# GpSimd takes part of the weight and activation scaling at the start of a hybrid encoder block

## The chip, the cores and the metric

One Trainium2 (trn2) chip, one core of it. The metric is the device time of one execution in microseconds (us); the kernel before takes 1410.32 us, the median of three runs.

## What is computed

One layer of a bidirectional encoder over 2048 tokens of width 1024: RMS norm, one input projection, a Fourier branch and a dilated-attention branch, and one output projection. The change touches only the operands of the input projection.

```python
def reference(x, norm_w, w_in, q_norm_w, k_norm_w, w_fourier, w_out):
    ...
    h = x.astype(jnp.float32)
    ...
        hn = rms_norm(h, norm_w)
        proj = hn @ w_in.astype(jnp.float32)
        u_f, g_f, q, k, v, g_a = jnp.split(proj, SPLIT_POINTS, axis=-1)
        ...
        mixed = jnp.concatenate([y_f, y_a], axis=-1) @ w_out.astype(jnp.float32)
        h = h + mixed
    return h.astype(x.dtype)
```

## The kernel before

The projection keeps float32 accuracy with pairs of float16 numbers. Each normalized x is split into a high half (its float16 rounding) and a low half (what the rounding left), each weight too, and a product is three float16 matmuls: high by high, low by high, high by low. An item of the projection is one tile of 128 tokens against one weight block of 384 columns: 8 chunks of the contracted width by 3 products, 24 matmuls (`inproj`, L303 to L316). There are 12 such blocks (units) of 16 items each; item `t` of unit `u` runs in turn `i = 16u + t` of one long loop, which also carries the attention of earlier units.

At the start all operands have to be made. `x_sq` (L184) sums the squares of a row of x on ScalarE, `x_rs` (L194) makes the reciprocal root with a chain of ten dependent, tiny VectorE instructions (L107 to L114), `x_hi` (L209) scales an x tile to its high half `xhl`, `x_lo` (L217) makes the low half on VectorE from the float32 tile and the high half, `x_tr` (L225) transposes on TensorE and `x_ev` (L233) copies the transposed halves into `xT`, by ScalarE where tile number plus half is even and by VectorE otherwise. From tile 4 on the low half is transposed by a DMA instead (`x_dt`, L237). `w_prep` (L255) finds a power of two for a weight block, makes its high half `wh[:, 0]` chunk by chunk (L289, ScalarE) and the low half `wh[:, 1]` from it (L291, VectorE). Square roots go one tile at a time for tiles 0 to 3 and for two tiles at once from tile 4 on (`xgrp`).

The order is written out by hand: each engine works off its instructions in the order in which the program issues them. In turns 0, 1 and 2 the loop prepares x tiles 2, then 3, then 4 and 5 (L1132); in later turns one tile, three ahead of the item. After the item's 24 matmuls, `q_raw` and `q_v` (L323 to L332) move its result out of PSUM by ScalarE and VectorE, and `q_ss` (L342) sums squares on VectorE. GpSimd has no work between its set-up and turn 7, when it begins to scale q and k (L364, L365). In turns 1 to 3 the small instructions of `gains` (L156 to L168) are woven into the same VectorE order.

Of the kernel before, what the change touches and what calls it, by code (L numbers as in the profile page):

```python
# [16 lines left out]
AF = mybir.ActivationFunctionType  # L17
OP = mybir.AluOpType
# [74 lines left out]
class Kernel:  # L93
# [115 lines left out]
    def x_hi(self, r):  # L209
        nc = self.nc  # L210
        t = self.xtl(r)
        ri = self.x_ri(r)
        hl = [self.wk.tile([128, D], F16, name="xhl", tag="pp", bufs=4) for _ in range(2)]
        self.XH[r] = hl
        nc.scalar.activation(hl[0], t, AF.Copy, scale=ri)

    def x_lo(self, r):  # L217
        nc = self.nc
# [36 lines left out]
    def w_prep(self, u, nxt=False):  # L255
        nc = self.nc
        n = sum(x[1] for x in self.segs(u))
        wr = [self.WL.pop((u, k))[:, :n] for k in range(KT)]
        V, A = nc.vector, nc.scalar
        am8 = self.sm.tile([128, KT + 2], F32, name="am8", bufs=2)  # L260
        am = am8[:, KT + 1:KT + 2]
        nc.gpsimd.memset(am8[:, KT:KT + 1], 2.0 ** -58)
        for k in range(KT):
            V.tensor_reduce(am8[:, k:k + 1], wr[k], AX.X, OP.max, apply_absolute_value=True)
            yield
        V.tensor_tensor(am8[:, :KT], am8[:, :KT], self.nw, OP.mult)
        V.tensor_reduce(am, am8[:, :KT + 1], AX.X, OP.max, apply_absolute_value=True)
        yield
        pm = self.psm.tile([128, 512], F32, name="pm", tag="m")
        nc.tensor.matmul(pm[:, :128], am.to_broadcast([128, 128]), self.idf, start=True, stop=True)  # L270
        yield
        sb = self.sm.tile([128, 4], F32, name="scb", tag="scb", bufs=17)
        nws = self.sm.tile([128, KT], F32, name="nws", bufs=2)
        V.tensor_reduce(sb[:, 2:3], pm[:, :128], AX.X, OP.max)
        self.pow2(sb[:, 2:3], sb[:, 1:2], sb[:, 0:1])
        V.tensor_scalar(nws, self.nw, sb[:, 0:1], 8.0, op0=OP.mult, op1=OP.mult)
        V.tensor_scalar(sb[:, 0:1], sb[:, 0:1], 8.0, None, op0=OP.mult)
        V.tensor_scalar(sb[:, 1:2], sb[:, 1:2], 1.0 / 16, None, op0=OP.mult)
        V.scalar_tensor_tensor(sb[:, 2:3], sb[:, 0:1], EPS, sb[:, 0:1], op0=OP.mult, op1=OP.mult)
        V.tensor_scalar(sb[:, 3:4], sb[:, 1:2], 0.5, None, op0=OP.mult)  # L280
        if u < len(self.units):
            c, sp = self.units[u]
            V.tensor_copy(self.IS[:, sp // 2, c, sp % 2], sb[:, 1:2].to_broadcast([128, 2]))
        wh = self.wp.tile([128, 2, KT, 384], F16, name="wh", tag="wh", bufs=2)
        self.W[u] = wh, sb
        yield
        for k in range(KT + 1):
            if k < KT:
                A.activation(wh[:, 0, k, :n], wr[k], AF.Copy, scale=nws[:, k:k + 1])  # L289
            if k:  # L290
                V.scalar_tensor_tensor(wh[:, 1, k - 1, :n], wr[k - 1], nws[:, k - 1:k], wh[:, 0, k - 1, :n],  # L291
                                       op0=OP.mult, op1=OP.subtract)
                if nxt:
                    self.WQ.append((u + 1, k - 1))
            yield
# [1016 lines left out]
```

## Time and profile before

| | |
|---|---|
| median of 3 runs | 1410.32 us (1410.22 to 1411.82) |
| the profiled execution's own time | 1410.9 us |
| its span in the trace | 1409.1 us |
| TensorE busy | 1381.4 us (98%) |
| VectorE busy | 992.7 us (70%) |
| ScalarE busy | 748.7 us (53%) |
| GpSimd busy | 459.7 us (33%) |

The span is the time between the first and the last instruction of the trace; the execution's own time has 1.8 us more around it. A share of busy time is an average over the whole span. The change works in its first 45 us alone, so the stretches there are to be read, and what each engine waits for at their ends.

### The profile page before, as it was taken

Reading aid. Unit: us, or ns where it says so; the run is one execution under the profiler, and the core shown is the slowest. Engines: PE = TensorE matmul, PEld = TensorE weight load, DVE = VectorE, ACT = ScalarE, POOL = GpSimd, SP = SyncE. Lnnn points to the kernel's source line nnn. Section 1 sums busy time; section 2 is a strip of 40 time slices with the busy share of each in tenths; the row PEclk is TensorE's granted clock in tenths of the full one; section 3 lists DMA queues with packets and bytes.
Section 4 is the critical chain, followed back from the end, with each engine's and each line's share of the span. In section 5 each row is a group of like instructions: output and inputs, shape, how many; then the busy total and the mean of one; then the engine's idle time right before and its main releaser. Section 6 shows DMA issues by size and latency. Waiting matters only on the chain.

```text
span 1409.1 us, 27788 instructions
## 1 busy us (share of the span) xinstructions
PE 1381.4 (98%) x9506; PEld 1020.7 (72%) x9506; DVE 992.7 (70%) x3167; ACT 748.7 (53%) x2095; POOL 459.7 (33%) x639
## 2 busy tenths in 40 slices
PE   5999999999999999999999999999999999899998
PEld 3666666667777777778888888844448688788887
DVE  7888888878878888888887777744398887711111
ACT  6867767676757666666666565645213235410010
POOL 0255445444444444454433343320000101411110
PEclk9999999999999999999999999999999999999999
DMA  6876877786776767687766564545432526353432
GB/s 225 204 134 127 153 121 142 127 143 132 141 132 124 149 119 155 118 152 120 144 115 130 97 132 96 136 108 145 164 103 92 149 76 254 111 148 116 112 113 82
DMA packets 426829, 188.13 MB, mean 134 GB/s; under 512 B 320128, under 2 KB 410432, under 8 KB 426176
## 3 DMA queue, kind: packets, MB, share of 16 engines
q1 hardware_dynamic: 398084, 173.37, 56.3%
q10 hardware_dynamic: 28604, 13.00, 3.8%
q8 instruction: 74, 1.21, 0.4%
q14 instruction: 67, 0.55, 0.1%
HBM read 68.18 MB, written 29.76 MB: 70 GB/s over the span
## 4 chain that ended last, share of the span: by engine, by line
PE 82%; DVE 6%; issue 3%; DMA 3%; POOL 3%; ACT 2%; SPq 1%; POOLq 0%; DVEq 0%; ACTq 0%
PE psq L312 43%; PE py L948 13%; PE psq L574 12%; PE psq L590 5%; PE pS L461 3%; PE po L527 2%; PE po L528 1%; PE pS L449 1%; DVE xhl L223 1%; POOL ph L509 1%; DMA qw<-qw 1%; PE pf L828 1%; DMA wor<-in_w_out_dram 1%; POOL hl L376 1%; PE ptr L795 0%
## 5 line engine op out<-in xcount | busy, mean ns | idle before, releaser
L312 PE MATMUL psq<-wh,xT 128*128 128x384 f16 x4608 | 787.0, 327 | 3.3 <-ACT wh L289 1.5
L312 PEld LDWEIGHTS <-xT 128*128 128x128 f16 x4608 | 540.3, 119 | 193.8 <-issue 4.6
L497 ACT ACTIVATE P<-pS,ob,kb 128x256 f32<-128x256 f32 (+1 forms) x384 | 199.4, 527 | 150.5 <-DVE ob L489 150.1
L509 POOL TENSOR_TENSOR ph<-P,ph 128x512 f16<-128x512 f32 x160 | 189.5, 1184 | 196.4 <-ACT ph L504 184.1
L948 PE MATMUL py<-wo,mx 128*128 128x512 f32 x768 | 180.1, 397 | 3.8 <-DVE mx L927 3.8
L365 POOL TENSOR_TENSOR qn<-qn,kb 128x128 f32<-128x128 f32 x192 | 85.6, 446 | 293.7 <-DVE qn L364 201.9
L948 PEld LDWEIGHTS py<-wo,mx 128*128 128x128 f32 x768 | 146.1, 190 | 37.6 <-DVE mx L927 4.2
L574 PE MATMUL psq<-xT,wh 128*128 128x512 f16 x768 | 168.9, 379 | 0.0
L479 DVE CUSTOM_DVE_ANT_0 pS<-pS,bt 128x256 f32<-128x256 f32 (+1 forms) x384 | 147.7, 385 | 27.3 <-PE pS L449 18.8
L376 POOL TENSOR_TENSOR hl<-qn,hl 128x256 f16<-128x256 f32 x192 | 133.4, 695 | 29.7 <-ACT hl L371 29.7
L574 PEld LDWEIGHTS <-wh 128*128 128x128 f16 x768 | 74.1, 98 | 87.0 <-issue 0.8
L951 DVE TENSOR_TENSOR xo<-xo,py 128x512 f32<-128x512 f32 x32 | 22.0, 686 | 144.1 <-PE py L948 144.1
L538 DVE TENSOR_REDUCE ob<-po 128x128 f32<-128x256 f32 (+1 forms) x160 | 75.2, 470 | 54.1 <-PE po L528 54.1
L504 ACT CAST ph<-P 128x512 f16<-128x512 f32 x160 | 99.1, 619 | 9.4 <-DMA wr<-in_w_in_dram 1.6
L371 ACT CAST hl<-qn 128x256 f16<-128x256 f32 x192 | 77.1, 402 | 47.3 <-POOL qn L365 37.5
L332 DVE TENSOR_TENSOR vt<-psq,vt 128x128 f16<-128x128 f32 x192 | 55.0, 286 | 62.0 <-ACT vt L331 61.8
L331 ACT CAST vt<-psq 128x128 f16<-128x128 f32 x192 | 51.2, 267 | 82.8 <-PE po L528 82.8
L291 DVE SCALAR_TENSOR_TENSOR wh<-wr,nws,wh 128x384 f16<-128x384 f32 x128 | 86.5, 682 | 5.5 <-ACT wh L289 5.5
L590 PE MATMUL psq<-wh,xT 128*128 128x256 f16 x768 | 84.3, 273 | 0.0
L926 ACT CAST mx<-ya 128x512 fp32r<-128x512 f16 x16 | 9.9, 620 | 137.5 <-PE py L948 131.6
L590 PEld LDWEIGHTS <-xT 128*128 128x128 f16 x768 | 75.1, 98 | 9.1
L323 ACT COPY raw<-psq 128x256 f32<-128x256 f32 x192 | 69.4, 361 | 21.8 <-PE psq L312 21.4
(165 smaller groups left out, 1773.2 us busy)
## 6 DMA issues: line engine op xcount, KB each, us to landing
wr<-in_w_in_dram SPq DMA_DIRECT2D x104, 192.0 KB, 2.9
ot<-O SPq DMA_DIRECT2D x16, 792.0 KB, 4.5
st<-st SPq DMA_DIRECT2D x96, 128.0 KB, 2.4
xs<-in_x_dram SPq DMA_DIRECT2D x16, 512.0 KB, 6.9
xo<-in_x_dram SPq DMA_DIRECT2D x16, 512.0 KB, 3.6
out_dram<-xo SPq DMA_DIRECT2D x15, 512.0 KB, 3.0
O<-ob ACTq DMA_DIRECT2D x108, 66.0 KB, 2.5
O<-ob ACTq DMA_DIRECT2D x32, 132.0 KB, 2.7
```

The lines of the kernel that those rows point to most:

```text
L291: V.scalar_tensor_tensor(wh[:, 1, k - 1, :n], wr[k - 1], nws[:, k - 1:k], wh[:, 0, k - 1, :n], op0=OP.mult, op1=OP.subtract)
L312: nc.tensor.matmul(ps[:, :384], self.xtile(j, k, c, t), wh[:, l, k, :384], start=n == 0, stop=n == 23)
L365: G.tensor_tensor(qn[:, 2:4], qn[:, 2:4], self.kf[:, h0:h0 + 2], OP.mult)
L371: self.nc.scalar.copy(hl.rearrange("p a h l d -> p (a h) l d")[:, :, 0], qn)
L376: self.nc.gpsimd.tensor_tensor(hv[:, :, 1], qn, hv[:, :, 0], OP.subtract)
L479: V.tensor_tensor_reduce(out=sS[:, h, cs], in0=ps[:, h, cs], in1=bs, scale=1.0, scalar=-3.0e38, op0=OP.add, op1=OP.max, accum_out=mx[:, e, ...
L497: self.nc.scalar.activation(P[:, h, cs], sS[:, h, cs], AF.Exp, bias=ob[:, e, 130 + h:131 + h], scale=self.om[:, h0 + h:h0 + h + 1], accum_ ...
L504: self.nc.scalar.copy(ph[:, 0], P)
L509: self.nc.gpsimd.tensor_tensor(ph[:, 1], P, ph[:, 0], OP.subtract)
L574: nc.tensor.matmul(ps, wh[:, l, k, col * 128:col * 128 + 128], self.xT[:, j, k, ch * 512:ch * 512 + 512], start=n == 0, stop=n == 23)
L590: nc.tensor.matmul(ps[:, j * 256:j * 256 + 256], self.xT[:, i, k, r * 128:r * 128 + 128], wh[:, l, k, 128:384], start=n % 24 == 0, stop=n ...
L948: nc.tensor.matmul(ps[nh], m[:, j, k], wo[nh][k][:, l], start=(j, l, k) == (0, 0, 4), stop=(j, k) == (1, 3))
```

## The change

Two of the places that make a high half get a second engine. In `x_hi`, tiles 2 to 5 are scaled by GpSimd and no longer by ScalarE. In `w_prep`, for unit 0 alone, the odd chunks (four of eight) are scaled by GpSimd. Sizes, types and results stay as they were, and nothing else is edited.

```diff
@@ x_hi
         self.XH[r] = hl
-        nc.scalar.activation(hl[0], t, AF.Copy, scale=ri)
+        if 2 <= r < 6:
+            nc.gpsimd.tensor_scalar(hl[0], t, ri, None, op0=OP.mult)
+        else:
+            nc.scalar.activation(hl[0], t, AF.Copy, scale=ri)
@@ w_prep
             if k < KT:
-                A.activation(wh[:, 0, k, :n], wr[k], AF.Copy, scale=nws[:, k:k + 1])
+                if u == 0 and k % 2:
+                    nc.gpsimd.tensor_scalar(wh[:, 0, k, :n], wr[k], nws[:, k:k + 1], None, op0=OP.mult)
+                else:
+                    A.activation(wh[:, 0, k, :n], wr[k], AF.Copy, scale=nws[:, k:k + 1])
```

The added lines move the numbers of later ones: L215, L223, L235, L289, L291, L364 before are L218, L226, L238, L295, L297, L370 after.

On GpSimd, from the set-up to the first scaling of q, the order before is this (`am` belongs to the search for the power of two, `qn` to q and k):

```order
masks.py:199 AFFINE_SELECT idf<-idf 128x128
L262 MEMSET am_160 128x1
L364 TENSOR_TENSOR qn<-raw,qny 128x256
L365 TENSOR_TENSOR qn<-qn,kb 128x128
L376 TENSOR_TENSOR hl<-qn,hl 128x4x64
```

and in the change:

```order
masks.py:199 AFFINE_SELECT idf<-idf 128x128
L265 MEMSET am_160 128x1
L293 TENSOR_SCALAR wh<-wr,nws 128x384 x4
L216 TENSOR_SCALAR xhl<-xs,xri 128x1024 x4
L370 TENSOR_TENSOR qn<-raw,qny 128x256
L371 TENSOR_TENSOR qn<-qn,kb 128x128
L382 TENSOR_TENSOR hl<-qn,hl 128x4x64
```

Eight instructions stand where there were none; the later ones follow in the same order.

On ScalarE, from the first weight chunk to item 0's `vt`, the order before is this (`xjk` is `x_sq`; the first `xhl` row is tile 1, the second tile 2):

```order
L289 ACTIVATE wh<-wr,nws 128x384 x2
L192 ACTIVATE xjk,xss<-xs 128x1024
L289 ACTIVATE wh<-wr,nws 128x384 x6
L215 ACTIVATE xhl<-xs,xri 128x1024
L192 ACTIVATE xjk,xss<-xs 128x1024
L235 COPY xT<-xps 128x8x128
L192 ACTIVATE xjk,xss<-xs 128x1024
L215 ACTIVATE xhl<-xs,xri 128x1024
L192 ACTIVATE xjk,xss<-xs 128x1024 x2
L323 COPY raw<-psq 128x256
L324 ACTIVATE sq<-psq 128x256
L331 CAST vt<-psq 128x128
```

and in the change:

```order
L295 ACTIVATE wh<-wr,nws 128x384
L192 ACTIVATE xjk,xss<-xs 128x1024
L295 ACTIVATE wh<-wr,nws 128x384 x3
L218 ACTIVATE xhl<-xs,xri 128x1024
L192 ACTIVATE xjk,xss<-xs 128x1024
L238 COPY xT<-xps 128x8x128
L192 ACTIVATE xjk,xss<-xs 128x1024 x3
L329 COPY raw<-psq 128x256
L330 ACTIVATE sq<-psq 128x256
L337 CAST vt<-psq 128x128
```

Four chunks and tile 2 are gone from ScalarE; item 0's `raw`, `sq` and `vt` stand behind one x tile less.

Further on ScalarE, from there to the copy of tile 3's low half into `xT`, the order before is this (`xhl` is tile 3, then tiles 4 and 5; the `xT` rows are tile 2's high half and tile 3's low half):

```order
L331 CAST vt<-psq 128x128
L215 ACTIVATE xhl<-xs,xri 128x1024
L235 COPY xT<-xps 128x8x128
L192 ACTIVATE xjk,xss<-xs 128x1024 x2
L323 COPY raw<-psq 128x256
L324 ACTIVATE sq<-psq 128x256
L331 CAST vt<-psq 128x128
L215 ACTIVATE xhl<-xs,xri 128x1024 x2
L235 COPY xT<-xps 128x8x128
```

and in the change:

```order
L337 CAST vt<-psq 128x128
L238 COPY xT<-xps 128x8x128
L192 ACTIVATE xjk,xss<-xs 128x1024 x2
L329 COPY raw<-psq 128x256
L330 ACTIVATE sq<-psq 128x256
L337 CAST vt<-psq 128x128
L238 COPY xT<-xps 128x8x128
```

Both `xT` copies move up directly behind `vt`, since tile 3 and tiles 4 and 5 are gone. The orders of VectorE and TensorE are the same in both kernels.

## Rows read from the trace of the kernel before

**Rows 1.** The page's head and its first part: busy time of each engine.

```profile
span 1409.1 us, 27788 instructions
PE 1381.4 (98%) x9506; PEld 1020.7 (72%) x9506; DVE 992.7 (70%) x3167; ACT 748.7 (53%) x2095; POOL 459.7 (33%) x639
```

**Rows 2.** Busy time of each engine in stretches from 15 to 60 us.

```profile
15.00:30.00 15.00, 12.71 (x76) 6.82 (x75) 13.16 (x50) 13.23 (x25) 0.00 (x0) 1.00 0.69 278
30.00:45.00 15.00, 13.38 (x106) 8.29 (x105) 12.80 (x48) 13.97 (x25) 0.00 (x0) 1.00 0.56 147
45.00:60.00 15.00, 15.00 (x112) 9.62 (x110) 13.37 (x47) 11.88 (x24) 5.00 (x7) 1.00 1.16 264
```

**Rows 3.** Timeline of TensorE and its weight loads: start, duration, [idle before, releaser].

```profile
31.88 0.34 PE L312 MATMUL psq<-wh,xT 128*128 128x384 f16 x1 [0.83 <-ACT xT L235]
37.97 1.96 PE L312 MATMUL psq<-wh,xT 128*128 128x384 f16 x11 [0.62 <-ACT xT L235]
42.57 1.82 PEld L312 LDWEIGHTS <-xT 128*128 128x128 f16 x12 [0.18 <-ACT xT L235]
45.06 4.06 PE L312 MATMUL psq<-wh,xT 128*128 128x384 f16 x24
```

**Rows 4.** What TensorE waited for from 45 to 1240 us: total, times, longest.

```profile
PE py L948 <- DVE mx L927: 3.8, 1, 3.8
PE pS L461 <- DMA qw<-qw: 3.1, 6, 0.6
PE po L527 <- DMA pt<-ph: 0.6, 1, 0.6
```

**Rows 5.** Timeline of VectorE, 15 to 37 us.

```profile
15.00 0.16 DVE L279 SCALAR_TENSOR_TENSOR scb<-scb 128x1 f32<-128x1 f32 x1
15.81 1.14 DVE L291 SCALAR_TENSOR_TENSOR wh<-wr,nws,wh 128x384 f16<-128x384 f32 x2
25.76 0.16 DVE L114 SCALAR_TENSOR_TENSOR xri<-xn1t,xri 128x1 f32<-128x1 f32 x1
27.14 1.28 DVE L223 SCALAR_TENSOR_TENSOR xhl<-xs,xri,xhl 128x1024 f16<-128x1024 f32 x1 [0.38 <-ACT xhl L215]
29.91 0.29 DVE L332 TENSOR_TENSOR vt<-psq,vt 128x128 f16<-128x128 f32 x1 [0.44 <-ACT vt L331]
30.18 0.21 DVE L156 TENSOR_TENSOR kw<-kw,kt 24x64 f32<-24x64 f32 x1
34.64 0.16 DVE L114 SCALAR_TENSOR_TENSOR xri<-xn2t,xri 128x2 f32<-128x2 f32 x1
35.71 0.16 DVE L112 SCALAR_TENSOR_TENSOR xn2t<-xn2t,xss 128x2 f32<-128x2 f32 x1
35.98 0.68 DVE L235 COPY xT<-xps 128x1024 f16<-128x1024 f16 x1
36.58 2.47 DVE L223 SCALAR_TENSOR_TENSOR xhl<-xs,xri,xhl 128x1024 f16<-128x1024 f32 x2
```

**Rows 6.** Timeline of ScalarE, 14 to 41 us.

```profile
14.82 1.12 ACT L289 ACTIVATE wh<-wr,nws 128x384 f16<-128x384 f32 x2 [2.31 <-DVE nws L276]
34.83 2.19 ACT L215 ACTIVATE xhl<-xs,xri 128x1024 f16<-128x1024 f32 x2 [0.22 <-DVE xri L114]
40.47 1.15 ACT L215 ACTIVATE xhl<-xs,xri 128x1024 f16<-128x1024 f32 x1 [0.80 <-PE xps L230]
```

**Rows 7.** GpSimd and VectorE side by side at 75 us.

```profile
75.20 0.60 POOL L364 TENSOR_TENSOR qn<-raw,qny 128x256 f32<-128x256 f32 x1
75.29 0.54 DVE L112 SCALAR_TENSOR_TENSOR xn2t<-xn2t,xss 128x2 f32<-128x2 f32 x1
```

**Rows 8.** GpSimd's groups by shape: busy us, mean ns of one.

```profile
L509 POOL TENSOR_TENSOR ph<-P,ph 128x512 f16<-128x512 f32 x160 | 189.5, 1184 | 196.4 <-ACT ph L504 184.1 <-issue 10.0 <-DMA O<-ob 2.3
L365 POOL TENSOR_TENSOR qn<-qn,kb 128x128 f32<-128x128 f32 x192 | 85.6, 446 | 293.7 <-DVE qn L364 201.9 <-DVE qny L114 65.6 <-DVE qnt L110 21.2
L262 POOL MEMSET am<- 128x1 f32 x16 | 1.6, 97 | 0.0
masks.py:199 POOL TENSOR_SCALAR_AFFINE_SELECT idf<-idf 128x128 f32<-128x128 f32 x1 | 0.3, 292 | 0.1
masks.py:197 POOL MEMSET idf<- 128x128 f32 x1 | 0.2, 204 | 0.3 <-POOLq L1302 0.3
```

## The prediction, made before the changed kernel ran

> **What bounds the kernel now.** I read the engines' shares first, then the stretches of the start, then what TensorE waits for, and last VectorE's and ScalarE's timelines up to 45 us. TensorE is busy 98% of the span [rows 1] and from 45 us on in every microsecond: 15.00 of 15 [rows 2]. Behind that point it waits only for short things that are themselves paced by the items (3.8, 3.1 and 0.6 us in all) [rows 4]. So whatever the start loses or wins by the moment item 4 begins, at 42.57 us [rows 3], is carried to the end one to one.
>
> Before that moment TensorE waits, and the last to end each wait is a copy into `xT` by ScalarE: 0.83 us at 31.88, 0.62 at 37.97, 0.18 at 42.57 [rows 3]. That speaks for taking work from ScalarE, which is busy 13.23 and 13.97 of 15 us [rows 2]. But VectorE is as full, 13.16 and 12.80 of 15, and its few named waits for ScalarE in 15 to 37 us are 0.38 and 0.44 us [rows 5]. There are two bounds side by side, and the change relieves one of them.
>
> The reader should then look at how GpSimd and VectorE stand to each other. At 75 us GpSimd's L364 starts at 75.20 and ends at 75.80; VectorE's L112, tiny and 0.16 us long at 35.71 [rows 5], starts at 75.29 and takes 0.54 [rows 7]. Its own work thus began at 75.29 + 0.54 - 0.16 = 75.67, that is 0.13 us before GpSimd's end. VectorE instructions with two inputs in SBUF and GpSimd instructions exclude each other, from start to about 0.13 before the end. GpSimd has 0.00 us in 15 to 45 us now [rows 2], so VectorE is free of this there. All root chains, `x_lo` and the low halves of the weights are such two-input instructions.
>
> **The price of the new instructions.** No row shows GpSimd scaling one tensor by a column. From below: MEMSET, 97 ns for one column and 204 for 128 [rows 8], is 0.84 ns a column, so 0.42 us for 384 columns and 0.95 for 1024. From above: the two-input instruction, 446 ns for 128 columns and 1184 for 512 [rows 8], is 1.92 ns a column on a fixed 0.20, so 0.94 and 2.17. In between stands AFFINE_SELECT, one tensor in and one out, 292 ns for 128 columns: from MEMSET's 97 it is 1.5 ns a column, so 0.68 and 1.64; on the fixed 0.20 of the two-input line it is 0.7. I take 0.95 ns a column on 0.20, half of the two-input slope: t = 0.56 us for 384 and T = 1.2 us for 1024. ScalarE takes 2.19 for two of 1024 [rows 6], so the move itself costs next to nothing; the exclusion is the cost.
>
> The Trainium skill, GPSIMD Engine Reference, section 4.1, says that GpSimd's one-input elementwise instructions run at roughly line rate; with its 1.2 GHz that is an estimate of 0.85 us for 1024 columns, and with it the sum below would be about +0.7 us. The trace's AFFINE_SELECT, 0.7 to 1.5 ns a column, leaves it open; no other row here has one input.
>
> **The change, step by step,** as the delay of VectorE, which keeps its order.
>
> 1. Weight chunks. ScalarE's first two take 1.12 us from 14.82 [rows 6]; GpSimd's four start about 14.86, all inputs being there. L279 at 15.00 [rows 5] has two SBUF inputs and waits until 14.86 + 0.56 - 0.13 = 15.29: +0.29. The copy of `xT` behind it reads PSUM and runs beside chunk 3. The first low half, due at 15.81 + 0.29 = 16.10 [rows 5], meets chunk 5 (15.90 to 16.46) and starts at 16.33; chunk 7 goes between it and the second, which starts at 17.33 in place of 16.34. VectorE is **1.0 us** late. With t = 0.42 the same walk gives 0.4, with 0.94 it gives 2.3. ScalarE's four chunks less save nothing here: the root of tile 1 stands behind these low halves on VectorE.
>
> 2. Tile 2. Its root is ready at 25.92, the end of the L114 at 25.76 [rows 5]. GpSimd starts 0.07 later and holds VectorE until T - 0.06 behind the root. Three tiny two-input steps of tile 3's root stand ahead of `x_lo` and now come after, 0.58 us, so `x_lo` starts T + 0.52 behind the root. It was 27.14 - 25.92 = 1.22 [rows 5]. Late by T - 0.70 = **0.5**.
>
> 3. Tile 3. ScalarE, rid of tile 2, has `vt` ready early, so the 0.44 us wait before 29.91 [rows 5] falls away; `vt` reads PSUM and passes. Then L156, 30.18 [rows 5], waits for GpSimd until T - 0.06 behind tile 3's root, which is 29.91 - 0.44 = 29.47. Late by T - 0.77 = **0.43**, the gain of 0.44 already in it.
>
> 4. Tiles 4 and 5. The root is ready at 34.80, the end of the L114 at 34.64 [rows 5]. Two GpSimd instructions follow each other from 34.87 and hold VectorE's chain of the next root at two places; its L112, 35.71 [rows 5], starts at 34.70 + 2T. Late by 2T - 1.01 = **1.39**. The copy into `xT` behind it (35.98) and the two `x_lo` (36.58) are late by as much [rows 5].
>
> Together VectorE is 1.0 + 0.5 + 0.43 + 1.39 = 3.3 us late at 36 us. TensorE starts item 3 late by less, since ScalarE's copy is now early (the 0.62 wait at 37.97 goes). Item 4 hangs on tile 6's high half on ScalarE, which stands ahead of tile 4's copy there: it began at 40.47, 0.80 us of it waiting for TensorE [rows 6], while its root on VectorE came about 0.34 earlier. That slack is used up and 3.3 - 0.34 = **+3.0 us** is left. The transposing DMAs of the low halves follow `x_lo` and hide inside it. After item 4 nothing is added: the eight instructions are over before GpSimd's first old one, and TensorE sets the pace.
>
> The sum against the profiled execution is 1410.9 + 3.0 = 1413.9 us; the median of the runs is 0.6 below that execution, so 1413.3. With both prices at their lower ends it is 0.4 + 0.25 + 0.18 + 0.89 - 0.34 = +1.4, at the AFFINE_SELECT slope 1.3 + 0.94 + 0.87 + 2.27 - 0.34 = +5.0, at the two-input slope 2.3 + 1.47 + 1.4 + 3.33 - 0.34 = +8.2.
>
> **The rivals.**
>
> *VectorE is not held* (not slower). If a GpSimd instruction with one tensor input leaves VectorE its second reading port, or gives way at every meeting, only ScalarE's relief stays. Then VectorE wins 0.44 us at 29.91 and tile 3's copies no longer stand behind two high halves of 2.19 us [rows 6], but tile 6's root on VectorE, 0.34 before 40.47, then decides: -0.44 - 0.34 = -0.8 us, 1409.5. It decides from the point where the holds, 3.8 us in the sum above before the two gains of 0.44 and 0.34, fall under 0.8 us. For it: no row has a one-input GpSimd instruction beside a root chain. Against it: rows 7 show the hold plainly, and a read is a read.
>
> *Half of it is hidden.* GpSimd's chunks could fall beside the copy from PSUM and the single-input steps, and the two high halves of tiles 4 and 5 could hold at one place: steps 1 and 4 halve, 3.0 - 0.5 - 0.7 = +1.8 us, 1412.1.
>
> *GpSimd's pass is slow.* At T between 1.64 and 2.17 it is the price and not the meetings that counts, +5.0 to +8.2 us, 1415.3 to 1418.5. For it: every two-input row of GpSimd has this slope; against it: the instruction reads one tensor. The Trainium skill, same page, section 3.1, calls about 1.8 cycles an element the best case of a tight loop; at 1.2 GHz that is an estimate of 1.54 us for 1024 columns, and about +4.3 us by it. No run here shows this yet.
>
> **How the numbers follow.** A measurement of this kernel can tell about 0.2% from no change, 2.8 us. The forecast, holds with T from 0.95 to 1.64, gets 0.63; its middle, +3.0, is just above that line. Hidden by half gets 0.12, slow pass 0.12, not held 0.13. Of the forecast some 0.38 lies above 2.8 us, which with the slow pass makes slower 0.50. The rest of it, hidden and nearly all of not held make same 0.47; no case reaches -2.8, and 0.03 is left for what I overlook. The range runs from -0.8 (not held) to +5.7, between AFFINE_SELECT's slope and the slow pass's middle: 1409.5 to 1416.0, with about 0.1 left out above and less below.
>
> **What would show it.** GpSimd's four chunks near 0.56 us and four tiles near 1.2 us, longer where a VectorE instruction of two inputs runs; VectorE's second low half starting near 17.3, `x_lo` of tile 2 near 28.6, tile 3's copy by VectorE near 39.3; TensorE waiting at 32 and 37 us for VectorE and no longer for ScalarE; item 4 at about 45.6. An item 4 before 42 us, with root chains of undisturbed 0.16 us steps beside GpSimd, would make the forecast wrong; so would GpSimd tiles of 2 us, or new waits of TensorE behind 60 us.

## The result and the profile after

| | before | after |
|---|---|---|
| median of 5 runs of each, side by side | 1410.32 us (1410.22 to 1412.18) | 1418.38 us (1415.03 to 1420.14) |
| ratio | | 1.0051, 95% interval 1.0039 to 1.0063 |
| the profiled execution's own time | 1410.9 us | 1415.03 us |
| its span | 1409.1 us | 1413.2 us |
| item 4 starts | 42.57 us | 48.03 us |
| first weight scale `nws` starts | 14.55 us | 14.25 us |

The medians lie 8.1 us apart; the ratio of the runs makes the changed kernel slower by 0.51%, 7.2 us (5.5 to 8.9), where +3.0 us was forecast and the range ended at 1416.0. The profiled execution happens to be the quickest of its five runs. Executions start their first weight scale up to 1.2 us apart (14.22 to 15.40 us in the profiles of this study), so below the start of item 4 is counted from there: 28.02 us before, 33.78 after, **+5.76 us**.

The page's head and the stretches of the start, after (columns as in [rows 2]: stretch, its length, busy us and count of PE, PEld, DVE, ACT, POOL, then the granted clock, DMA share and GB/s):

```profile
span 1413.2 us, 27800 instructions
PE 1382.0 (98%) x9506; PEld 1020.2 (72%) x9506; DVE 997.9 (71%) x3167; ACT 743.3 (53%) x2087; POOL 479.3 (34%) x647
```

```profile
15.00:30.00 15.00, 12.39 (x60) 6.07 (x59) 12.78 (x42) 9.71 (x19) 7.76 (x5) 1.00 0.74 298
30.00:45.00 15.00, 11.72 (x98) 7.44 (x96) 12.57 (x43) 6.68 (x14) 8.55 (x3) 1.00 0.37 105
45.00:60.00 15.00, 13.04 (x97) 8.19 (x96) 12.18 (x46) 12.51 (x23) 2.86 (x3) 1.00 0.85 218
```

ScalarE went from 13.97 busy microseconds to 6.68 in the second stretch [rows 2], so it was relieved as meant. VectorE is hardly less busy than before and TensorE lost 1.66 us in that stretch. What follows 60 us did not change by more than execution to execution: TensorE's waits from 45 us on name the same tiles as [rows 4], with item 4's new wait among them.

GpSimd's groups by shape, after (busy us, mean ns of one):

```profile
L216 POOL TENSOR_SCALAR xhl<-xs,xri 128x1024 f16<-128x1024 f32 x4 | 11.4, 2853 | 12.1 <-DVE xss L200 6.7 <-DVE xri L114 5.5
L293 POOL TENSOR_SCALAR wh<-wr,nws 128x384 f16<-128x384 f32 x4 | 5.3, 1348 | 13.3 <-DMA xs<-in_x_dram 13.3
```

A tile takes 2.85 us and a chunk 1.35, against the 1.2 and 0.56 that I took, and above my upper bounds of 2.17 and 0.94 too.

GpSimd's timeline at the start, after (start, duration):

```profile
14.58 5.33 POOL L293 TENSOR_SCALAR wh<-wr,nws 128x384 f16<-128x384 f32 x4 [13.25 <-DMA xs<-in_x_dram]
26.60 2.85 POOL L216 TENSOR_SCALAR xhl<-xs,xri 128x1024 f16<-128x1024 f32 x1 [6.69 <-DVE xss L200]
32.06 2.87 POOL L216 TENSOR_SCALAR xhl<-xs,xri 128x1024 f16<-128x1024 f32 x1 [2.61 <-DVE xri L114]
37.76 5.68 POOL L216 TENSOR_SCALAR xhl<-xs,xri 128x1024 f16<-128x1024 f32 x2 [2.84 <-DVE xri L114]
```

VectorE's timeline beside it, after:

```profile
14.70 0.47 DVE L282 SCALAR_TENSOR_TENSOR scb<-scb 128x1 f32<-128x1 f32 x1
...
26.19 0.16 DVE L114 SCALAR_TENSOR_TENSOR xri<-xn1t,xri 128x1 f32<-128x1 f32 x1
...
26.82 0.91 DVE L110 TENSOR_TENSOR xn1t<-xri 128x1 f32<-128x1 f32 x1
27.76 0.16 DVE L112 SCALAR_TENSOR_TENSOR xn1t<-xn1t,xss 128x1 f32<-128x1 f32 x1
27.95 0.16 DVE L114 SCALAR_TENSOR_TENSOR xri<-xn1t,xri 128x1 f32<-128x1 f32 x1
29.48 1.28 DVE L226 SCALAR_TENSOR_TENSOR xhl<-xs,xri,xhl 128x1024 f16<-128x1024 f32 x1 [1.37 <-POOL xhl L216]
...
32.70 0.50 DVE L110 TENSOR_TENSOR xn2t<-xri 128x2 f32<-128x2 f32 x1
...
34.95 1.28 DVE L226 SCALAR_TENSOR_TENSOR xhl<-xs,xri,xhl 128x1024 f16<-128x1024 f32 x1 [0.46 <-POOL xhl L216]
...
38.23 0.67 DVE L110 TENSOR_TENSOR xn2t<-xri 128x2 f32<-128x2 f32 x1
...
40.66 2.13 DVE L226 SCALAR_TENSOR_TENSOR xhl<-xs,xri,xhl 128x1024 f16<-128x1024 f32 x1 [0.76 <-POOL xhl L216]
43.48 1.28 DVE L226 SCALAR_TENSOR_TENSOR xhl<-xs,xri,xhl 128x1024 f16<-128x1024 f32 x1 [0.69 <-POOL xhl L216]
44.68 0.15 DVE L110 TENSOR_TENSOR xn2t<-xri 128x2 f32<-128x2 f32 x1
```

Two different things are to be seen. First the **hold**: L110 at 26.82 takes 0.91 where the same step takes 0.16 undisturbed, so its own work began at 26.82 + 0.91 - 0.16 = 27.57, 0.97 us behind GpSimd's start. But GpSimd goes on until 29.45, and the two-input steps at 27.76 and 27.95 run beside it, undisturbed. The hold covers only the first third of the instruction. At L282, beside a chunk, the same reckoning gives 14.70 + 0.47 - 0.16 - 14.58 = 0.43 us. Second the **late result**: VectorE then has nothing to do but wait for the high half, 1.37, 0.46, 0.76 and 0.69 us before the four `x_lo`, each of which starts within 0.06 us of a GpSimd end. That is 3.28 us in all; before, only 0.38 us of such waiting stood there, for ScalarE at tile 2 [rows 5].

TensorE's timeline, after (the counterpart of [rows 3]; item 4 is the 48.03):

```profile
34.56 1.96 PE L318 MATMUL psq<-wh,xT 128*128 128x384 f16 x11 [1.00 <-DVE xT L238]
...
39.95 2.12 PE L318 MATMUL psq<-wh,xT 128*128 128x384 f16 x12 [0.59 <-DVE xT L238]
...
43.50 0.62 PE L233 MATMUL xps<-idh,xhl 128*128 128x128 f16 x8 [0.98 <-POOL xhl L216]
...
48.03 2.12 PE L318 MATMUL psq<-wh,xT 128*128 128x384 f16 x12 [1.96 <-ACT xT L238]
```

The waits for ScalarE of [rows 3] became waits for VectorE and GpSimd. The last one still names ScalarE, but only as messenger: its high half of tile 6 began at 45.93 after 5.72 us idle, waiting for tile 6's root on VectorE, and the copy behind it began at 46.99.

### The profile page after: what moved, and what is told of

Same layout as the page of the kernel before. It is cut to its first block, busy times and chain, and to the rows that moved or that the text cites. A ratio compares the mean times of both kernels' runs of the same rounds, so it can differ in the third digit from the quotient of the medians.

```text
span 1413.2 us, 27800 instructions
## 1 busy us (share of the span) xinstructions
PE 1382.0 (98%) x9506; PEld 1020.2 (72%) x9506; DVE 997.9 (71%) x3167; ACT 743.3 (53%) x2087; POOL 479.3 (34%) x647
## 4 chain that ended last, share of the span: by engine, by line
PE 80%; DVE 6%; DMA 4%; POOL 4%; issue 3%; ACT 1%; SPq 1%; POOLq 0%; ACTq 0%; DVEq 0%
PE psq L318 43%; PE py L954 13%; PE psq L580 12%; PE psq L596 5%; PE pS L467 3%; PE po L533 2%; PE po L534 1%; DMA Y<-SG 1%; POOL ph L515 1%; DMA pt<-ph 1%; DVE xhl L226 1%; PE pS L455 1%; POOL xhl L216 1%; DMA wor<-in_w_out_dram 1%; POOL hl L382 1%
## 5 line engine op out<-in xcount | busy, mean ns | idle before, releaser
L297 DVE SCALAR_TENSOR_TENSOR wh<-wr,nws,wh 128x384 f16<-128x384 f32 x128 | 86.8, 684 | 5.5 <-ACT wh L295 5.5
```

## Experiments

Each is counted as item 4's start behind `nws`, and as a ratio to the kernel before on the same chip, whose runs there had medians of 1410.59, 1410.35 and 1411.26 us.

| run | item 4 behind `nws` | median us | ratio, 95% interval |
|---|---|---|---|
| before | 28.02 | 1410.32 | 1 |
| r1_again | 33.79 | 1417.23 | 1.0051 (1.0039 to 1.0064) |
| r2_chunks | 28.74 | 1411.89 | 1.0009 (1.0000 to 1.0018) |
| r3_tiles | 33.08 | 1415.84 | 1.0037 (1.0024 to 1.0049) |
| r4_unread | 30.81 | 1413.51 | 1.0020 (1.0011 to 1.0029) |
| r5_twoinput | 33.98 | 1417.10 | 1.0045 (1.0033 to 1.0058) |
| r6_tile5 | 28.49 | 1410.66 | 1.0006 (0.9997 to 1.0015) |
| r7_filled | 33.77 | 1417.34 | 1.0053 (1.0040 to 1.0065) |
| r8_filled_before | as before | 1408.75 | 0.9988 (0.9979 to 0.9997) |
| r9_prices | as before | 1411.15, one run | |
| r10_split | 29.13 | 1413.30 | 1.0013 (1.0004 to 1.0023) |
| r11_tail_filled | 33.79 | 1415.16 | 1.0031 (1.0020 to 1.0043) |

**r1_again.** The changed kernel, unedited, beside the next three.

> The changed kernel as it is, once more, for the spread of its five runs (1415.0 to 1420.1 us, in steps of about 1.7). Theory A (late results: the trace's loss of 5.5 us at item 4 is all there is): item 4 again near 48.0 us, and the runs gather near 1415 to 1416. [...]

The loss is the same, 7.2 us by the ratio, and item 4 stands at the same place, 33.79; the runs gather near 1417 us, above the 1415 to 1416 of theory A. What differs from the first profile is TensorE's clock behind item 4's wait. TensorE's row in r1_again, and the stretches (length, PE busy, granted clock, DMA share, GB/s):

```profile
49.14 3.80 PE L318 MATMUL psq<-wh,xT 128*128 128x384 f16 x12 [1.97 <-ACT xT L238]
```

```profile
46.00:50.00 4.00, 2.04 (x12) 0.92 0.51 93
50.00:54.00 4.00, 4.00 (x23) 0.66 0.94 256
54.00:58.00 4.00, 4.00 (x32) 1.00 1.00 260
```

Item 4's first twelve matmuls took 3.80 us where they take 2.12 in the first profile after, 1.7 us more; the clock fell to the lower of its two levels for part of 46 to 54 us, behind a wait of 1.97 us. In the first profile after, a wait as long (1.96) was followed by clock 1.00. So this price is paid in some executions and not in others.

**r2_chunks and r3_tiles.** One half of the change each: r2 leaves `x_hi` as before, r3 leaves `w_prep` as before.

```diff
 r2: x_hi
-        if 2 <= r < 6:
-            nc.gpsimd.tensor_scalar(hl[0], t, ri, None, op0=OP.mult)
-        else:
-            nc.scalar.activation(hl[0], t, AF.Copy, scale=ri)
+        nc.scalar.activation(hl[0], t, AF.Copy, scale=ri)
 r3: w_prep
-                if u == 0 and k % 2:
-                    nc.gpsimd.tensor_scalar(wh[:, 0, k, :n], wr[k], nws[:, k:k + 1], None, op0=OP.mult)
-                else:
-                    A.activation(wh[:, 0, k, :n], wr[k], AF.Copy, scale=nws[:, k:k + 1])
+                A.activation(wh[:, 0, k, :n], wr[k], AF.Copy, scale=nws[:, k:k + 1])
```

> Only the weight chunks go to GpSimd; the x tiles stay on ScalarE. Theory A (VectorE and TensorE wait for GpSimd's late results): the chunks take 1.35 us each, 5.3 us for four, and all are there before their low halves' turn, so item 4 begins at most 0.5 us later than 42.57. Theory B (GpSimd's reading holds VectorE off): the same three or four holds of 0.2 to 0.5 us as in the changed kernel, item 4 0.5 to 1.0 later. By either the run is 1410.5 to 1411.5 us; 1413 or more would say that the chunks are a large part of the loss.

> Only the x tiles 2 to 5 go to GpSimd; the chunks stay on ScalarE. Theory A: VectorE's low halves wait for results that come 2.85 us after the root instead of 1.15, item 4 begins 4.5 to 5.5 us later than 42.57, near 47.5, and the time is 1415 us or more, almost all of the loss. Theory B: holds of about 0.9 us at four tiles, half of them hidden, item 4 only 2 us later.

The chunks cost 0.7 us at item 4 and the tiles 5.1; 0.7 + 5.1 = 5.8 is the whole. In time the medians lie 1.3 and 5.25 us above before, 6.55 together; that of r1_again lies 6.6 above (7.2 by its ratio). The parts add, and the tiles are nearly all of it.

**r4_unread.** The kernel before, with GpSimd making the same eight halves into a part of `xT` that is still unused then, where nothing reads them. ScalarE makes its halves as before.

```diff
 x_hi
         nc.scalar.activation(hl[0], t, AF.Copy, scale=ri)
+        if 2 <= r < 6:
+            nc.gpsimd.tensor_scalar(self.xT[:, 1, :, 1920:2048], t.rearrange("p (k n) -> p k n", n=128), ri, None, op0=OP.mult)
 w_prep
                 A.activation(wh[:, 0, k, :n], wr[k], AF.Copy, scale=nws[:, k:k + 1])
+                if u == 0 and k % 2:
+                    nc.gpsimd.tensor_scalar(self.xT[:, 1, 0:3, 1920:2048], wr[k].rearrange("p (k n) -> p k n", n=128), nws[:, k:k + 1], None, op0=OP.mult)
```

> The kernel before, in which GpSimd makes the same eight high halves a second time at the same places, into a part of xT that is written over later and that nobody reads before that; ScalarE's own are the ones that are used. So VectorE's reading port is held as in the change, but nothing waits for GpSimd's results and ScalarE has all its work. Theory A: item 4 near 42.6 to 43.2, time within 1 us of before. Theory B (the holds are the cost, as forecast): item 4 near 44.5 to 45.5, time 2 to 3 us above before.

GpSimd's presence alone, with nobody waiting for what it makes, puts item 4 off by 2.8 us and the kernel by 2.9. The other 3.0 of 5.8 us comes only when the result is needed. VectorE's timeline in r4_unread, where GpSimd's tiles started at 26.89, 30.82 and 36.64:

```profile
27.03 0.99 DVE L110 TENSOR_TENSOR xn1t<-xri 128x1 f32<-128x1 f32 x1
...
30.93 1.02 DVE L200 TENSOR_SCALAR xss<-xss 128x2 f32<-128x2 f32 x1
...
36.80 0.97 DVE L107 TENSOR_SCALAR xri<-xss 128x2 int32<-128x2 int32 x1
```

Each hold ends 0.97 us behind GpSimd's start (end less the undisturbed 0.16). And L200 and L107, which have one input, are held like those with two. GpSimd seems to be kept out by VectorE as well: its last two tiles took 7.53 us together in place of 5.68, while VectorE's two `x_lo` ran from 39.07 to 41.54, and tile 5's hold then fell on the root step behind them (L110 at 41.46, 0.99 us).

**r5_twoinput.** The tiles as a product of two inputs, the second a broadcast column.

```diff
-            nc.gpsimd.tensor_scalar(hl[0], t, ri, None, op0=OP.mult)
+            nc.gpsimd.tensor_tensor(hl[0], t, ri.to_broadcast([128, D]), OP.mult)
```

> The changed kernel, in which GpSimd makes tiles 2 to 5 by a product of two tensors (the root column broadcast) and not by a scalar column. By the rows of such products an instruction takes about 2.17 us in place of 2.85, but holds VectorE off for about 2.04 us of it in place of 0.98. Theory A (only the late result counts): item 4 begins about 2 us earlier against the power of two (nws) than in the changed kernel, 31.8 us behind it in place of 33.8, time 1 to 2 us lower. Theory B (the hold counts as well): the gain of 0.68 us a tile is given back at tile 3 and at tiles 4 and 5, where two holds stand in VectorE's chain; item 4 about 34 to 35 us behind nws, time as the changed kernel or 1 us more.

This instruction takes 1.90 us, less than the one with a single tensor input, and still item 4 is not earlier. GpSimd's and VectorE's timelines in r5_twoinput:

```profile
27.29 1.90 POOL L216 TENSOR_TENSOR xhl<-xs,xri 128x1024 f16<-128x1024 f32 x1 [6.67 <-PE psq L318]
```

```profile
27.53 1.67 DVE L110 TENSOR_TENSOR xn1t<-xri 128x1 f32<-128x1 f32 x1
...
29.52 1.28 DVE L226 SCALAR_TENSOR_TENSOR xhl<-xs,xri,xhl 128x1024 f16<-128x1024 f32 x1
...
32.17 1.85 DVE L107 TENSOR_SCALAR xri<-xss 128x2 int32<-128x2 int32 x1
...
38.62 1.83 DVE L107 TENSOR_SCALAR xri<-xss 128x2 int32<-128x2 int32 x1
...
40.69 1.60 DVE L110 TENSOR_TENSOR xn2t<-xri 128x2 f32<-128x2 f32 x1
```

Here the hold lasts nearly the whole instruction: L110's own work began at 27.53 + 1.67 - 0.16 = 29.04, 1.75 us behind GpSimd's start and 0.15 before its end, as in [rows 7]. `x_lo` no longer waits for GpSimd. At tile 2 that is a gain: `nws` starts at 14.96 in this run, so `x_lo` begins 14.56 us behind it, against 15.23 in the kernel after (29.48 - 14.25). The gain is given back at tile 3, where L107 is held for 1.85 us, and at tiles 4 and 5, where L107 and L110 are held for 1.83 and 1.60 one behind the other: what was won in latency is lost as a longer hold, as theory B had it.

**r6_tile5.** Only tile 5 on GpSimd, with `w_prep` as in r3_tiles, against which the edit is shown.

```diff
-        if 2 <= r < 6:
+        if r == 5:
```

> Only tile 5 goes to GpSimd, beside ScalarE's tile 4; the chunks and tiles 2, 3, 4 stay on ScalarE. Its 2.85 us run beside tile 4's low half, one hold of 0.3 us falls on VectorE's chain, and tile 3's copy on ScalarE comes 1 us earlier. Theory A and B alike: item 4 within 0.3 us of before (28.0 us behind nws), time as before. If ScalarE alone were the bound, item 4 would begin 0.5 to 0.8 us earlier.

Item 4 comes 0.5 us later, not earlier, and the time is the same as before within its interval. ScalarE had one tile less and stood idle for 2.42 us ahead of tile 6's high half at 40.62, with the root on VectorE the releaser. VectorE's timeline in r6_tile5, where GpSimd's tile started at 34.55:

```profile
34.69 1.00 DVE L107 TENSOR_SCALAR xri<-xss 128x2 int32<-128x2 int32 x1
```

So the run has one hold of 0.84 us (1.00 less 0.16) on that root's chain, and item 4 follows it. Item 3 did gain by the relief: the transposes behind it begin 24.86 us behind `nws` (39.09) in place of 25.22 (39.77). What taking work from ScalarE would be worth without any hold is not shown by this run.

**r9_prices.** Six forms alone in a quiet stretch of the output projection of the kernel before, on 1024 and on 384 columns that nothing else reads.

```diff
 ...
+                for n in (1024, 384):
+                    G.tensor_scalar(h[:, :n], src[:, :n], sc, None, op0=OP.mult)
+                    G.tensor_scalar(f[:, :n], src[:, :n], sc, None, op0=OP.mult)
+                    G.tensor_scalar(h[:, :n], src[:, :n], 1.0, None, op0=OP.mult)
+                    G.tensor_tensor(h[:, :n], src[:, :n], sc.to_broadcast([128, n]), OP.mult)
+                    G.tensor_tensor(h[:, :n], src[:, :n], src[:, :n], OP.mult)
+                    G.tensor_copy(h[:, :n], src[:, :n])
```

> What makes GpSimd's pass 2.85 us long. The kernel before, with GpSimd alone in the quiet stretch of the output projection running six forms one after another, on 1024 and then 384 columns of float32 that nothing else reads: scalar column to float16, scalar column to float32, constant scalar to float16, two inputs with the second a broadcast column, two inputs that are both whole tensors, and a plain cast to float16. The outputs are unused. Theory P (the form with a scalar column is slow in itself): 2.85 and 1.35 us for both column forms, whatever the output type; 1.0 to 1.4 us for the cast; 1.9 us for the broadcast product, as in the run with two-input products. Rival Q (writing float16 is slow): the float32 output takes under 1.8 us and the cast about 2.8. Rival R (what is slow is VectorE's work beside it at the start, not the form): all of one input take about 1.2 us here, the two-input ones 1.2 to 1.9. Time: the added GpSimd work is off the path, within 0.2% of before.

GpSimd's groups of this run, by shape (busy us, mean ns):

```profile
L1298 POOL TENSOR_SCALAR zh<-zs,zc 128x1024 f16<-128x1024 f32 x1 | 2.8, 2849 | 0.1
L1299 POOL TENSOR_SCALAR zf<-zs,zc 128x1024 f32<-128x1024 f32 x1 | 2.8, 2846 | 0.0
L1300 POOL TENSOR_SCALAR zh<-zs 128x1024 f16<-128x1024 f32 x1 | 2.8, 2770 | 0.0
L1301 POOL TENSOR_TENSOR zh<-zs,zc 128x1024 f16<-128x1024 f32 x1 | 1.9, 1939 | 0.1
L1302 POOL TENSOR_TENSOR zh<-zs 128x1024 f16<-128x1024 f32 x1 | 1.9, 1894 | 0.1
L1298 POOL TENSOR_SCALAR zh<-zs,zc 128x384 f16<-128x384 f32 x1 | 1.2, 1242 | 0.1
L1303 POOL CAST zh<-zs 128x1024 f16<-128x1024 f32 x1 | 1.0, 1036 | 0.1
L1303 POOL CAST zh<-zs 128x384 f16<-128x384 f32 x1 | 0.5, 502 | 0.1
```

The form itself is slow: 2.85 us, the same with float32 out, when no VectorE instruction ran beside it, and 2.77 with a constant for the column, where theory P had named the column. A cast of the same tile takes 1.04 and a product of two whole tensors 1.89. My guess of 1.2 us was right for a cast, and not for this instruction. The holds of 0.43 us (384 columns) and 0.98 (1024) are close to the casts' 0.50 and 1.04; why the rest of the instruction leaves VectorE's two-input steps alone is not shown.

**r10_split.** Each tile shared by the two engines.

```diff
-            nc.gpsimd.tensor_scalar(hl[0], t, ri, None, op0=OP.mult)
+            nc.gpsimd.tensor_scalar(hl[0][:, 512:], t[:, 512:], ri, None, op0=OP.mult)
+            nc.scalar.activation(hl[0][:, :512], t[:, :512], AF.Copy, scale=ri)
```

> The changed kernel, but each of tiles 2 to 5 shared: GpSimd scales columns 512 to 1023, ScalarE columns 0 to 511. Theory A (about half of the loss is that the high half comes late, 2.85 us after the root): GpSimd's pieces take about 0.45 + 512 * 2.35 ns = 1.65 us, 1.2 us less, and nearly all of the part put down to lateness, 3.0 us at item 4, goes, while the holds at each start stay: item 4 starts 30.5 to 32 us after the first weight scale is there (33.8 in the changed kernel, 28.0 before, 30.8 with the same work unread). Theory B (the holds alone, which grow with the work done): the holds halve, and item 4 falls to about 29.5. Rival C (ScalarE as the bound, since it now runs eight pieces in place of four): item 4 stays at 33 or later. Time by A about 1413 to 1415, by B 1411.5 to 1412.5, by C 1416 or more.

Item 4 stands at 29.13, +1.1 us, below what A gave and nearest to B. GpSimd's and VectorE's timelines in r10_split say why:

```profile
26.57 1.56 POOL L216 TENSOR_SCALAR xhl<-xs,xri 128x512 f16<-128x512 f32 x1 [6.69 <-DVE xri L107]
```

```profile
26.80 0.47 DVE L112 SCALAR_TENSOR_TENSOR xn1t<-xn1t,xss 128x1 f32<-128x1 f32 x1
...
28.17 1.28 DVE L227 SCALAR_TENSOR_TENSOR xhl<-xs,xri,xhl 128x1024 f16<-128x1024 f32 x1 [0.71 <-POOL xhl L216]
```

With half the columns the hold ends 26.80 + 0.47 - 0.16 - 26.57 = 0.54 us behind the start, and `x_lo` starts 1.3 us sooner than in the kernel after. I had expected the holds to stay; they follow the columns. Both parts shrink, so this run does not tell them apart. It shows that 4.65 of the 5.76 us go when GpSimd has half a tile, and still the kernel is 1.8 us slower than before (0.6 to 3.2).

**r7_filled, r8_filled_before and r11_tail_filled.** Unread matmuls put into TensorE's waits, 14 ahead of the output projection (r8: in the kernel before; r11: in the kernel after), and in r7 also 12 before item 4.

```diff
+        fl = self.psm.tile([128, 512], F32, name="fl", tag="m")
+        for _ in range(14):
+            self.nc.tensor.matmul(fl, wo[0][0][:, 0, :128], wo[0][0][:, 0], start=True, stop=True)
 r7, in the long loop
+                if i == 4:
+                    fl = self.psm.tile([128, 512], F32, name="fl", tag="m")
+                    for _ in range(12):
+                        nc.tensor.matmul(fl[:, :384], self.xT[:, 0, 0, 0:128], self.W[0][0][:, 0, 0, :384], start=True, stop=True)
```

> The changed kernel with matmuls whose result nobody reads in two waits of TensorE: 12 of 384 columns before item 4 and 14 of 512 columns before the output projection. Theory C (the waits cost clock as well): no stretch at half clock behind either wait, and the five runs lie within 2 us and 2 to 4 us below the changed kernel's, 1413 to 1415.5. Theory A alone: the same 1416 to 1418 as before, since the waits are only filled; and if the fillers are longer than the waits, up to 1 us more.

> The kernel before with the 14 unread matmuls in the wait ahead of the output projection alone (it was 3.75 us, and 6.8 us at half clock followed). Theory C: no half clock there, 1407 to 1408.5 us, 1.7 to 3.4 below before, and a smaller spread. Without it: as before, 1410.6, or 0.5 more if the filler outlasts the wait.

> The changed kernel with 14 unread matmuls ahead of the output projection alone, none before item 4. Theory D (TensorE's half clock behind the wait there costs some 1.6 us in it, as it did in the kernel before): 1.0 to 2.0 us under the changed kernel's runs, 1415.5 to 1417; output projection at granted clock 1.0 throughout. Theory E (the run with both fillers gained nothing because the changed kernel's half clock is short there and the filler takes its time back): within 0.7 us of the changed kernel. The loss at the start, 5.8 us at item 4, stays by both.

In the kernel before, TensorE waits 3.75 us ahead of the output projection and comes back at the lower level (length, PE busy, granted clock, DMA share, GB/s, before):

```profile
1226.00:1230.00 4.00, 4.00 (x10) 0.50 0.02 4
1230.00:1234.00 4.00, 4.00 (x16) 0.80 0.96 220
```

In r8_filled_before the wait is 0.65 us, and the same stretches are:

```profile
1226.00:1230.00 4.00, 4.00 (x19) 1.00 0.12 15
1230.00:1234.00 4.00, 4.00 (x19) 1.00 0.83 234
```

That is 1.6 us faster than the kernel before (0.4 to 3.0), the quickest version of this study. In the kernel after, the same filler (r11) brings the median to 1415.16, some 2 us under r1_again, and granted clock 1.00 to the whole tail. By its ratio 4.4 us remain, near the 5.8 of item 4 less the 1.6 that the filler is worth. With the filler before item 4 as well (r7), the granted clock is 1.00 throughout, yet the time is that of the kernel after: the run has new waits of TensorE's matmuls, 0.7 us for `am` at 78.8 us and 1.0 for `wh` behind 1000 us, which the profiles of the kernel after, of r1_again and of r11 do not have. Also 2.45 us of its time at the median lie outside its span, 1.8 in r11. Whether the extra PSUM tile of the filler makes these was not tried, so what the half clock behind item 4 costs on average stays open; the one row that shows it says 1.7 us.

## Why the prediction was wrong

The direction, the place and the carriage to the end were right. Item 4 is where the loss shows, TensorE waits for VectorE and no longer for ScalarE at 34.56 and 39.95, and nothing was added later by the eight instructions. Two rows of VectorE's timeline before are needed beside [rows 5] and [rows 6]:

```profile
32.25 1.26 DVE L223 SCALAR_TENSOR_TENSOR xhl<-xs,xri,xhl 128x1024 f16<-128x1024 f32 x1
...
38.97 0.15 DVE L110 TENSOR_TENSOR xn2t<-xri 128x2 f32<-128x2 f32 x1
```

Step by step, as delay against `nws`:

| step | forecast | measured | from |
|---|---|---|---|
| 1. chunks | +1.0 | +0.73 | tile 2's root: L114 25.76 [rows 5], 26.19 after, `nws` 0.30 earlier |
| 2. tile 2 | +0.5 | +1.91 | its `x_lo` 27.14 [rows 5], 29.48 after |
| 3. tile 3 | +0.43 | +0.36 | its `x_lo` 32.25 before, 34.95 after |
| 4. tiles 4 and 5, to tile 4's `x_lo` | +1.39 | +1.38 | 36.58 [rows 5], 40.66 after |
| (not in the sum) tile 5's `x_lo` | 0 | +1.63 | the L110 behind it, 38.97 before, 44.68 after |
| slack at tile 6 | -0.34 | -0.25 | `x_hi` of tile 6, 40.47 [rows 6], 45.93 after |
| item 4 | +3.0 | +5.76 | |

**The step that failed is "The price of the new instructions".** I took T = 1.2 us and called 2.17, the two-input line of [rows 8], the upper end, because one input cannot cost more than two. It can: 2.85 us here, and 2.85 alone in r9. The Trainium skill, GPSIMD Engine Reference, section 4.1, has one-input elementwise work at roughly line rate; the cast's 1.04 us agrees, the scaling by a column at 2.85 does not.

**A second assumption failed beside it,** that hold and duration are one number. The Trainium skill, SBUF — State Buffer, section "Who interferes with whom", says of VectorE's two-port modes that whichever engine issues first gets the ports shared with GpSimd for the whole instruction. The two-input product agrees (1.75 of 1.90 us in r5, and [rows 7]); the scaling does not, 0.98 of 2.85. With holds as long as the measured T, steps 2 to 4 alone would come to 2.15 + 2.08 + 4.69 = 8.9 us, more than the whole loss: the two errors pull against each other. The holds that I had worked out from T were nearly right by chance: T - 0.13 = 1.07 us against 0.98, and 0.43 against 0.43 for a chunk. That is why step 1 came out close, and why r4, with holds alone, lost 2.8 us.

Steps 3 and 4 came out close by luck. I had made them of holds alone, one and two. What the timeline after shows is a smaller hold on the root chain, 0.35 and 0.52 us (L110 at 32.70 and 38.23 takes 0.50 and 0.67, undisturbed 0.15), and then a wait for the high half, 0.46 and 0.76 us. The other hold that I had put into step 4 fell on tile 4's `x_lo`.

What I had no term for is the result, which is there only at 2.85 us. VectorE waits for it at all four `x_lo`. Tile 2's starts 3.13 us behind its root (29.48 - 26.35) in place of the forecast 1.7; tile 5's waits 0.69 us behind one that is itself held for 0.85 (2.13 in place of 1.28); tiles 3 and 4 hide most of it behind the next root's steps. The four waits, less the 0.38 us of before, are 2.9 us, and r4 leaves 3.0 of the 5.76 to the late result: two ways to the same size.

**The rivals.** "GpSimd's pass is slow", at 0.12, had the time (1415.3 to 1418.5) and the cause, a slow pass; not its mechanism, since the longer pass is a wait for data and not a longer hold, so that its time is partly luck. "VectorE is not held" is refuted by r4. "Half of it is hidden" is not seen: step 1 cost 0.73, and the hold that left step 4 came back at tile 4's `x_lo`. Whether ScalarE is a second bound beside VectorE, as I read [rows 3], stays open: in r6 its relief brought item 3's end 0.36 us forward, and a hold on VectorE put item 4 back by 0.5.

**Outside the sum** stands TensorE's clock. It had no term in mine, and r1_again shows 1.7 us of it at the start in one execution. The 5.76 us at item 4 and the 7.2 us of the ratio differ by 1.4, which this could fill; it lies within the interval (5.5 to 8.9), and is not shown to be that. In the two profiled executions the loss even shrinks towards the end: it is 5.46 us at item 4 by the trace's own zero (42.57 and 48.03), 5.13 where the output projection's long run of matmuls begins (1225.96 and 1231.09) and 4.1 in the span. That last run takes 179.49 us before, 178.49 after, and 176.9 at granted clock 1.00 in r8 and r11. So the middle carries the loss nearly one to one, and how long the clock is low behind the wait there differs from execution to execution.

## What to carry to other kernels

An idle engine's instruction has two prices, how long it keeps a neighbour's instructions out and when its result is there; ask of each consumer on the path which of the two it meets. Price the very form that will run: a neighbouring form with more operands is no upper bound, and one run of the six forms in a quiet stretch would have settled here what the rows before could not. When work leaves an engine that shows up as last releaser, ask what that engine will wait for once the work is gone: ScalarE was named at three waits before, and without its tiles it stood idle behind VectorE's root chain, 2.42 us in r6 and 5.72 in the kernel after.

## What the hardware showed that I had not expected

- On GpSimd a multiplication by a scalar, column or constant, takes 2.85 or 2.77 us for 1024 columns and 1.24 or 1.17 for 384 (r9), 1.5 times the product of two tensors (1.89, 0.83).
- It keeps VectorE's instructions out for 0.43, 0.54 and 0.98 us at 384, 512 and 1024 columns, about a third of its length; the two-input product does so to 0.15 us before its end.
- VectorE instructions with one input of two columns in SBUF are held as well: L107 and L200 in r4_unread (0.97 and 1.02 us in place of 0.16). I had counted two-input ones alone.
- The hold begins a little behind GpSimd's start: L107 passed undisturbed 0.07 us behind it in the kernel after (32.13 and 37.83, 0.16 and 0.17 us), and L200 was held 0.11 behind it in r4_unread (30.93).
- Near its end the scaling is not without effect either: L164, one input of 24x64, took 0.54 in place of 0.24 us in r4_unread, 2.35 us behind GpSimd's start; why is not shown, and the copy behind it was not late.
- Behind waits as short as 2 us TensorE may come back at its lower clock level (r1_again, 1.97 us), or not (the first profile after, 1.96 us).
